# The split probabilities of a windowed attention laid side by side, the first operand of an output projection made earlier, and loads moved

## The chip, the cores and the metric

The kernel runs on one core of a Trainium2 chip. Its metric is the device time of one execution in microseconds (us), as the median of several runs; the slowest core counts, and here there is only one.

## The reference, cut to what matters

One layer of a hybrid encoder for 2048 prompt tokens and 64 decode tokens, 1024 wide. Attention (8 heads in 2 groups of 4, heads 64 wide, in chunks of 64 tokens, each of which sees its own chunk and the two before it) and a retention (4 heads, 128 wide) read one projection of the normed input. Their outputs go through one output projection, and a squared-ReLU MLP follows.

```python
a = _rmsnorm(hp, norm1[l])
qa, ka, va, qr, kr, vr, gr = _project(a, w_in[l], pos_p)      # rotates qa, ka, qr, kr
attn_o = _swa_prompt(qa, ka, va, sinks[l])
ret_o, s_p = _retention_prompt(qr, kr, vr)
hp = hp + _mix_out(attn_o, ret_o, gr, w_out[l])
hp = hp + _sqrelu_mlp(_rmsnorm(hp, norm2[l]), w_up[l], w_down[l])
...
def _attend(q, k, v, sinks, mask):
    s = jnp.einsum('...qkgd,...skd->...kgqs', q, k).astype(jnp.float32) * (HEAD_DIM ** -0.5)
    ...
    m = jnp.maximum(jnp.max(s, axis=-1), sink)
    p = jnp.exp(s - m[..., None])
    denom = jnp.sum(p, axis=-1) + jnp.exp(sink - m)
    p = (p / denom[..., None]).astype(v.dtype)
    o = jnp.einsum('...kgqs,...skd->...qkgd', p, v)
```

The attention has a band: for a tile of 128 tokens (two chunks) the keys are those of the tile before and of the tile itself, 256 columns, of which chunk 0 sees columns 0 to 192 and chunk 1 columns 64 to 256.

## The kernel before

All products are made from split operands: a float32 value is written as a high part that the fast matmul format holds exactly, and a low part, the rest. ScalarE (ACT) makes the high part by a copy, VectorE (DVE) the low part by a subtraction, and three matmuls per 128 rows of depth take the place of one. What the names mean: `xh` and `xl` are the split x, `w_1_1_5` is the split weight block 5 of column group 1 in the second phase, `raw`, `wraw` and `waraw` are weight blocks as loaded, `z` is the projection of a tile.

The first stage runs over 17 tiles (16 of 128 prompt tokens, and the decode tile of 64, whose low part lies beside the high one, so that it takes two matmuls per depth) in two phases, each for one half of the heads: in a phase every tile goes through three column groups of 384, 512 and 512 columns (`CN`). Group 0 holds the attention's values, keys and queries, groups 1 and 2 the retention's. The decode tile and the first prompt tile are done first, group by group in turn. The loop at L658 to L690 walks the groups; `group` (L549) issues the 24 (16) matmuls of one.

Behind the groups run the stages of the attention, `att_a` to `att_e` (L240 to L354): rotation and split of values and queries into `hl` (a value block is 128 columns, high and low parts beside each other), the transposes of queries and keys (`pq`, `pk`, into `qT` and `kw`), scores and softmax (`att_c`, L274), the transposes of the probabilities into `pt` and their split into `ph` and `pl` (`att_d`, L321), and the product with the values into `po` (`att_e`, L339). `att_c` writes the probabilities of a chunk at their place among the 256 columns and clears the 64 columns that the chunk doesn't see; `att_d` transposes all 256 columns of both chunks and both head pairs, that is eight blocks of 128 x 128 in two PSUM tiles. The retention stages are `ret_*`: `qk` is its rotated input, `ptr` the transposes of it, copied to `rkT`; `pss` are its scores, `pr` its product, `sd` its state, and `vs` and `sig` its values and gate.

The order of work on TensorE (PE) and on the DMA queue of SyncE (SP) is that in which the code issues it (L583); on the other engines a scheduler arranges it by a simulation of their times. A planner (`run_ready`, L531) puts the attention and retention stages between the matmuls of the groups: a stage is ready a time `LAT` after the stages that it needs, and adds `COST` to its clock. Nearly all loads go out on SP's queue, one behind the other, each waiting until its buffer is free and the eighth load before it has landed.

The start (L585 to L621) warms PE with 18 matmuls and issues the loads of the first group's weights (`load_w`, L115), of the x parts of the first two tiles (`load_part`, L591), of the second group's weights, of `rd`, of the token-wise x for the norm (`xk`) and the rotation table (`rt`, `load_aux`), and of the third group's weights, whose last loads borrow buffers of the attention stages, `ph` and `pl`. `token_norm` (L180) computes a tile's norm factor from `xk`.

At the change of phase, `load_ahead` (L123) loads the first blocks of a column group's next weights before the last group that uses the old ones, and `weights` splits them behind it. `load_x` (L146) loads a tile's x into `xr`, a single buffer, which GpSimd (POOL) leaves last, when it has made `xl`. Tile (1, 1) is the first of the second phase that is loaded anew; its load is issued at the group with the number `change + 7`.

The output projection (`out_part`, L764) forms eight blocks of 128 output columns d from eight blocks of mixed heads, in passes over 704 tokens, two halves of 352 each: 24 matmuls `y` per half. `wo` is the split operand, loaded and split one block ahead by `load_wout` (L754); `mhl` are the split mixed heads. Its first pass starts while the last tiles' attention is still under way: `run_ready` stands before each depth step until `phase1_done` (L852), which empties the stage queue. It is called behind the second output block (d = 1), by the hooks at L863.

## Time and profile before

| | |
|---|---|
| median of 3 runs | 2221.25 us (2221.06 to 2223.52) |
| profiled execution | 2221.45 us |
| its span | 2219.7 us |
| instructions | 35656 |
| VectorE busy | 1466.4 us (66%) |
| ScalarE busy | 1115.6 us (50%) |
| GpSimd busy | 444.8 us (20%) |
| mean DMA rate over the span | 232 GB/s |

The span runs from the first to the last instruction of the profiled execution; what lies around it makes the rest of its time. An engine's busy time is the sum of its instructions; two engines may be busy at once, so these times don't add up. The largest groups of instructions are TensorE's matmuls of the MLP, which stand behind the output projection and are not touched by the change.

### The profile page before, as it was taken

The numbers are of one execution on the slowest core, as the hardware profiler recorded it, in microseconds if no ns is written. First come the engines' busy times: TensorE is split into PE (matmuls) and PEld (weight loads), VectorE is DVE, ScalarE is ACT, GpSimd is POOL, SyncE is SP. The second block draws the span as 40 slices with busy tenths as digits, with TensorE's granted clock in tenths as the row PEclk, the third lists the DMA queues.
The fourth block names the chain that finished last, engine by engine and source line by source line (L and its number), as shares of the span: only waits on it lengthen the run. The fifth ranks groups of instructions, "written<-read, shape, count | busy, mean of one in ns | idle before, by whom it ended". The sixth has DMA issues, their size and how long they took to land.

```text
span 2219.7 us, 35656 instructions
## 1 busy us (share of the span) xinstructions
PE 2196.7 (99%) x13274; PEld 2108.1 (95%) x13274; DVE 1466.4 (66%) x2461; ACT 1115.6 (50%) x1983; POOL 444.8 (20%) x547
## 2 busy tenths in 40 slices
PE   8999999999999999999999999999999999999998
PEld 7888898888888999999999999999999999999998
DVE  6565557555456576787688668667666876677664
ACT  6444445444444433455565556555554444554452
POOL 4554444444443212100000000000001200120011
PEclk9999999999999999999999999999999999999999
DMA  6567964598554779489799779676976787777662
GB/s 184 163 182 186 249 173 151 166 221 204 138 124 132 263 264 336 151 306 347 237 322 350 258 234 323 228 231 215 361 263 226 269 290 239 234 275 271 239 211 81
DMA packets 240878, 515.92 MB, mean 232 GB/s; under 512 B 20144, under 2 KB 126320, under 8 KB 236608
## 3 DMA queue, kind: packets, MB, share of 16 engines
q1 hardware_dynamic: 231616, 469.62, 62.4%
q0 software_dynamic: 8512, 43.29, 9.3%
q8 instruction: 104, 1.70, 0.3%
q10 hardware_dynamic: 576, 0.72, 0.1%
q14 instruction: 70, 0.57, 0.1%
HBM read 411.19 MB, written 169.54 MB: 262 GB/s over the span
## 4 chain that ended last, share of the span: by engine, by line
PE 95%; DMA 2%; DVE 1%; issue 1%; ACT 1%; SPq 0%; POOL 0%; DVEq 0%; ACTq 0%; POOLq 0%
PE y L1094 9%; PE y L1093 9%; PE y L1092 9%; PE z L559 7%; PE z L560 7%; PE z L562 7%; PE b L922 4%; PE b L921 4%; PE b L920 4%; PE y L783 3%; PE y L785 3%; PE y L784 3%; PE a L922 3%; PE a L921 3%; PE a L920 3%; PE c L922 3%
## 5 line engine op out<-in xcount | busy, mean ns | idle before, releaser
L1094 PE MATMUL y<-vh,wd 128*128 128x352 f32 x1344 | 434.5, 323 | 0.5 <-DVE wd L496 0.5
L1093 PE MATMUL y<-vl,wd 128*128 128x352 f32 x1344 | 433.8, 323 | 0.0
L1092 PE MATMUL y<-vh,wd 128*128 128x352 f32 x1344 | 431.9, 321 | 0.0
L559 PE MATMUL z<-w,xh 128*128 128x512 f32 (+1 forms) x816 | 324.9, 398 | 1.4 <-ACT w L88 1.1
L1042 POOL TENSOR_TENSOR acc<-acc,sq 128x352 f32<-128x352 f32 x41 | 72.0, 1756 | 1212.2 <-ACT sq L1038 1212.2
L560 PE MATMUL z<-w,xh 128*128 128x512 f32 (+1 forms) x816 | 308.4, 378 | 1.1 <-DVE w L89 1.1
L495 ACT ACTIVATE wd<-dr 128x1024 fp32r<-128x1024 f32 x168 | 177.5, 1057 | 249.4 <-PE y L1094 171.7
L495 ACT ACTIVATE wu<-upr 128x512 fp32r<-128x512 f32 x336 | 209.2, 627 | 177.0 <-PE b L922 87.3
L562 PE MATMUL z<-w,xl 128*128 128x512 f32 (+1 forms) x768 | 288.9, 376 | 0.1
L496 DVE TENSOR_TENSOR wu<-upr,wu 128x512 fp32r<-128x512 f32 x336 | 231.2, 694 | 70.7 <-ACT wu L495 56.5
L496 DVE TENSOR_TENSOR wd<-dr,wd 128x1024 fp32r<-128x1024 f32 x168 | 209.2, 1247 | 95.6 <-ACT wd L495 95.6
L1094 PEld LDWEIGHTS y<-vh,wd 128*128 128x128 f32 x1344 | 252.8, 188 | 0.8 <-DVE wd L496 0.8
L1092 PEld LDWEIGHTS y<-vh,wd 128*128 128x128 f32 x1344 | 252.4, 188 | 0.0
L1093 PEld LDWEIGHTS y<-vl,wd 128*128 128x128 f32 x1344 | 252.4, 188 | 0.0
L921 PE MATMUL b<-al,wu 128*128 128x352 f32 x576 | 186.0, 323 | 0.0
L922 PE MATMUL b<-ah,wu 128*128 128x352 f32 x576 | 185.7, 323 | 0.0
L920 PE MATMUL b<-ah,wu 128*128 128x352 f32 x576 | 185.1, 322 | 0.0
L560 PEld LDWEIGHTS z<-w,xh 128*128 128x128 f32 x816 | 156.4, 192 | 20.6 <-DVE w L89 3.7
L559 PEld LDWEIGHTS z<-w,xh 128*128 128x128 f32 x816 | 156.4, 192 | 19.0 <-ACT w L88 1.6
L496 DVE TENSOR_TENSOR vl<-rv,vh 128x1408 fp32r<-128x1408 f32 x84 | 138.2, 1647 | 44.3 <-ACT vh L495 43.8
L562 PEld LDWEIGHTS z<-w,xl 128*128 128x128 f32 x768 | 145.0, 189 | 22.1 <-DVE xl L164 0.4
L495 ACT ACTIVATE vh<-rv 128x1408 fp32r<-128x1408 f32 x84 | 116.1, 1382 | 62.1 <-DMA rv<-vscr 44.9
(289 smaller groups left out, 4731.6 us busy)
## 6 DMA issues: line engine op xcount, KB each, us to landing
rv<-vscr SPq DMA_DIRECT2D x84, 704.0 KB, 5.5
vscr<-C SPq DMA_DIRECT2D x48, 1056.0 KB, 5.7
upr<-uscr SPq DMA_DIRECT2D x192, 256.0 KB, 5.1
dr<-sscr SPq DMA_DIRECT2D x96, 512.0 KB, 4.7
upr<-in_wup SPq DMA_DIRECT2D x144, 256.0 KB, 3.6
dr<-in_wdn SPq DMA_DIRECT2D x72, 512.0 KB, 5.2
uscr<-in_wup POOLq DMA_DIRECT2D x16, 1024.0 KB, 9.5
sscr<-in_wdn POOLq DMA_DIRECT2D x16, 1024.0 KB, 8.9
```

What stands on the lines that cost most here:

```text
L495: nc.scalar.activation(h, x, AF.Copy)
L496: nc.vector.tensor_sub(l, x, h.bitcast(F32))
L559: nc.tensor.matmul(z[:, :n], xh[:, k], wh, start=k == 0, stop=False)
L560: nc.tensor.matmul(z[:, :n], xh[:, k], wl, start=False, stop=k == NK - 1 and xl is None)
L562: nc.tensor.matmul(z[:, :n], xl[:, k], wh, start=False, stop=k == NK - 1)
L920: nc.tensor.matmul(o, wh, ah[:, k], start=k == 0 and i in (1, 6, 5), stop=False, skip_group_check=True)
L921: nc.tensor.matmul(o, wh, al[:, k], start=False, stop=False, skip_group_check=True)
L922: nc.tensor.matmul(o, wl, ah[:, k], start=False, stop=k == 3 and i in (2, 4, 3), skip_group_check=True)
L1042: nc.gpsimd.tensor_add(self.acc, self.acc, sq)
L1092: nc.tensor.matmul(o, wh, vh, start=f == 0, stop=False)
L1093: nc.tensor.matmul(o, wh, vl, start=False, stop=False)
L1094: nc.tensor.matmul(o, wl, vh, start=False, stop=f == 15)
```

## The change

**Attention.** The probabilities `p` of a head pair now lie in 384 columns, chunk 0 in 0 to 192 and chunk 1 in 192 to 384, so that there are no unseen columns, and the two memsets go. Three transposes of 128 columns serve a head pair instead of four: the first 128 columns (chunk 0 with the tile before), the last 128 (chunk 1 with this tile), and the middle 128, in which the upper 64 rows of the transpose belong to chunk 0 and the lower 64 to chunk 1. The former two go to `pt`, the middle one to `pm`. The middle rows are split in halves: in the new tile `pm`, one half of the 128 partitions holds the high part and the other the low part. A new tile `vd` holds the matching 64 rows of the values twice, once in each half of the partitions, made in `att_a` by copies on ACT and DVE. `att_e` now forms each chunk's `po` from three matmuls of 256 columns instead of both chunks' from four of 512. The planner's `COST` of `att_d` and `att_e` is lowered.

**Start.** The loads of the gains and of the decode tile's two x parts go out on ACT's DMA queue; on SP's queue all eight weight loads of the second group stand before `xk`, `rt` and `rd`. The borrowed buffers of the third group's loads are now one of `ph`, `pl`, `pm` and `p` each.

**Phase change.** The load of tile (1, 1)'s x is issued right behind `load_ahead(1)`.

**Output projection.** The first `wo` is loaded and split behind the last use of the second column group in phase 1, into buffers that the x tiles used (`xl`, `xk`, and `xr` for the raw load). `phase1_done` is called behind the third output block instead of the second.

```diff
-    nc.sync.dma_start(gsb, gains)
+    nc.scalar.dma_start(gsb, gains)
...
-            wk.tile([128, 512], F32, name="waraw", tag=tag, bufs=2) if tag else \
+            wk.tile([128, 2, 384 if tag == "p" else 256], F32, name="waraw", tag=tag).rearrange("p a n -> p (a n)") if tag else \
...
+        c.vd_prev = att[ph, t - 1].vd if 0 < t < NT - 1 else None
+        vd = c.vd = wk.tile([128, 2, 128], F32R, name="vd", bufs=3)
...
+        for a in range(c.nch):
+            v = hl[64 * a:64 * a + 64, 0:128].bitcast(F32)
+            nc.scalar.activation(vd[64 * (1 - a):128 - 64 * a, a], v, AF.Copy)
+            nc.vector.tensor_copy(vd[64 * a:64 * a + 64, a], v)
...
-        p = a.p = wk.tile([128, 2, 2, 256], F32, name="p")
+        p = a.p = wk.tile([128, 2, 384], F32, name="p")
...
-        if t > 0:
-            nc.gpsimd.memset(p[:, 0, :, 192:256], 0.0)
-            nc.gpsimd.memset(p[:, 1, :, 0:64], 0.0)
-        else:
-            nc.gpsimd.memset(p[:, 0, :, 192:256], 0.0)
...
     def att_d(a):
-        a.parts = []
-        nu = 2 * a.nch
-        for j in range(0 if a.t > 0 else 1, 2):
-            K = 128 if j == 0 else a.T
-            pt = psum("pt")
-            for c in range(a.nch):
-                for pr in range(2):
-                    v = 2 * c + pr
-                    nc.tensor.transpose(pt[:K, v * 128:v * 128 + 128], a.p[:, c, pr, j * 128:j * 128 + K], idf)
-            th = wk.tile([128, 512], F32R, name="ph", bufs=2)
-            tl = wk.tile([128, 512], F32R, name="pl", bufs=2)
-            nc.scalar.activation(th[:K, :nu * 128], pt[:K, :nu * 128], AF.Copy)
-            nc.vector.tensor_sub(tl[:K, :nu * 128], pt[:K, :nu * 128], th[:K, :nu * 128].bitcast(F32))
-            vv = (a.hl_prev if j == 0 else a.hl)[:K, 0:128]
-            a.parts.append((vv, th[:K, :nu * 128]))
-            a.parts.append((vv, tl[:K, :nu * 128]))
+        a.parts = [[], []]
+        n, t = a.nch, a.t
+        full = [c for c in range(n) if c == 1 or t > 0]
+        f0, f1 = full[0] * 256, full[-1] * 256 + 256
+        K = 128 if n == 2 and t > 0 else 64
+        pt, pm = psum("pt"), psum("pm")
+        for c in full:
+            for pr in range(2):
+                v = 2 * c + pr
+                nc.tensor.transpose(pt[:, v * 128:v * 128 + 128], a.p[:, pr, 256 * c:256 * c + 128], idf)
+        for pr in range(2):
+            nc.tensor.transpose(pm[:K, pr * 128:pr * 128 + 128], a.p[:, pr, 128:128 + K], idf)
+        th = wk.tile([128, 512], F32R, name="ph")
+        tl = wk.tile([128, 512], F32R, name="pl")
+        tm = wk.tile([128, 2, 256], F32R, name="pm")
+        nc.scalar.activation(th[:, f0:f1], pt[:, f0:f1], AF.Copy)
+        nc.vector.tensor_sub(tl[:, f0:f1], pt[:, f0:f1], th[:, f0:f1].bitcast(F32))
+        for c in full:
+            vv = (a.hl if c else a.hl_prev)[:, 0:128]
+            a.parts[c] += [(vv, x[:, 256 * c:256 * c + 256]) for x in (th, tl)]
+        for c in range(K // 64):
+            h, l = tm[64 * c:64 * c + 64, c], tm[64 * (1 - c):128 - 64 * c, c]
+            x = pm[64 * c:64 * c + 64, 0:256]
+            nc.scalar.activation(h, x, AF.Copy)
+            nc.vector.tensor_sub(l, x, h.bitcast(F32))
+            a.parts[c].append(((a.vd_prev if c else a.vd)[:, c], tm[:, c]))
 
     def att_e(a):
...
-        for i, (l, r) in enumerate(a.parts):
-            nc.tensor.matmul(po[:, :nu * 128], l, r, start=i == 0, stop=i == len(a.parts) - 1)
+        for c in range(nch):
+            for i, (l, r) in enumerate(a.parts[c]):
+                nc.tensor.matmul(po[:, 256 * c:256 * c + 256], l, r, start=i == 0, stop=i == len(a.parts[c]) - 1)
...
-    COST = dict(att_b=0.35, att_c=0.85, att_d=0.88, att_e=0.86, ret_b=0.44, ret_c=0.44, ret_d=1.3, ret_e=0.22)
+    COST = dict(att_b=0.35, att_c=0.85, att_d=0.66, att_e=0.72, ret_b=0.44, ret_c=0.44, ret_d=1.3, ret_e=0.22)
...
-        nc.sync.dma_start(xraw[n][:, k:k + 4, :T], xt[:, k:k + 4, t0:t0 + T] if T == 128 else xd[:, k:k + 4])
-
-    raws = []
-    for k in range(NK):
-        raws.append(load_w(0, 0, k, True))
-        if k < 2:
-            load_part(0, 4 * k)
+        (nc.sync if n else nc.scalar).dma_start(xraw[n][:, k:k + 4, :T], xt[:, k:k + 4, t0:t0 + T] if T == 128 else xd[:, k:k + 4])
+
+    for k in range(2):
+        load_part(0, 4 * k)
...
+    raws = [load_w(0, 0, k, True) for k in range(NK)]
...
-    raws = [load_w(0, 1, k, True) for k in range(4)]
+    raws = [load_w(0, 1, k, True) for k in range(NK)]
+    xs[a] = [*x0, load_aux(*a)]
     nc.sync.dma_start(rd, rdec)
-    xs[a] = [*x0, load_aux(*a)]
-    raws += [load_w(0, 1, k, True) for k in range(4, NK)]
...
-    raws = [load_w(0, 2, k, tag=(None, None, None, "ph", "ph", "pl", "pl")[k]) for k in range(NK - 1)]
+    raws = [load_w(0, 2, k, tag=(None, None, None, "ph", "pl", "pm", "p")[k]) for k in range(NK - 1)]
...
             raws = load_ahead(ci)
+            if ci == 1:
+                n = len(xs)
+                assert tiles[n] == (1, 1) and n not in xraw
+                xraw[n] = load_x(1)
...
+            raw = xp.tile([128, 1024], F32, name="wo0raw", tag="xr", bufs=1)
+            nc.sync.dma_start(raw, wout[0])
+            for a in range(2):
+                w = xp.tile([128, 2, 512], F32R, name="wo0", tag=("xl", "xk")[a], bufs=2 - a)
+                first_wo.append((w[:, 0], w[:, 1]))
+            for a in range(2):
+                split(*first_wo[a], raw[:, a * 512:a * 512 + 512])
...
-    wnext.append(load_wout(0))
+    wnext.append(first_wo)
     hooks = {d: [later(next_mix, 1, 2 * (d - 2) + k) for k in range(2)] for d in range(2, 6)}
-    hooks[1] = [phase1_done]
+    hooks[2].insert(0, phase1_done)
```

How instructions stand on an engine is shown at three places; a row gives the line, the operation, out<-in, and partitions x elements, with x and a count for rows in a series.

SP's queue at the start, in the kernel before (`gsb` are the gains, `xr` x for the matmuls, `xd` that of the decode tile, `xk` x by tokens for the norm):

```order
L63 DMA gsb<-in_gains 128x24
L120 DMA wraw<-in_w 128x384
L593 DMA xr<-in_xd 128x256
L120 DMA wraw<-in_w 128x384
L593 DMA xr<-in_xd 128x256
L120 DMA wraw<-in_w 128x384 x6
L593 DMA xr<-in_xt 128x4x128 x2
L120 DMA wraw<-in_w 128x512 x4
L607 DMA rd<-in_rdec 128x8
L172 DMA xk<-in_xtok 64x1024
L174 DMA rt<-in_rot 64x384
L120 DMA wraw<-in_w 128x512 x4
```

And in the changed kernel:

```order
L118 DMA wraw<-in_w 128x384 x8
L608 DMA xr<-in_xt 128x4x128 x2
L118 DMA wraw<-in_w 128x512 x8
L170 DMA xk<-in_xtok 64x1024
L172 DMA rt<-in_rot 64x384
L623 DMA rd<-in_rdec 128x8
L118 DMA raw<-in_w 128x512 x3
L118 DMA waraw<-in_w 128x512 x4
```

The gains and the decode tile's x parts have left the queue; the eight 128x512 loads stand together, and `xk`, `rt` and `rd` behind them, where `xk` stood in their middle. Those three loads stand at the head of ACT's order in the changed kernel, ahead of its first computation:

```order
L63 DMA gsb<-in_gains 128x24
L608 DMA xr<-in_xd 128x256 x2
L613 ACT_TABLE_LOAD
L613 ACTIVATE first<-mhalf 128x3
L86 ACTIVATE w_0_0_0_154<-wraw,gsb 128x384
L161 ACTIVATE xh<-xr 128x4x64
```

SP's queue at the change of phase, before:

```order
L120 DMA raw<-in_w 128x384 x8
L120 DMA raw<-in_w 128x512 x3
L128 DMA xk<-in_w 128x2x512
L120 DMA raw<-in_w 128x512 x3
L152 DMA xr<-in_xt 128x8x128
L120 DMA raw<-in_w 128x512 x3
L128 DMA xk<-in_w 128x2x512
L120 DMA raw<-in_w 128x512 x3
```

And in the changed kernel:

```order
L118 DMA raw<-in_w 128x384 x8
L118 DMA raw<-in_w 128x512 x3
L126 DMA xk<-in_w 128x2x512
L150 DMA xr<-in_xt 128x8x128
L118 DMA raw<-in_w 128x512 x6
L126 DMA xk<-in_w 128x2x512
L118 DMA raw<-in_w 128x512 x3
```

The x load (`xr`) stands right behind the load of two blocks at once (`xk<-in_w`) of the second column group, ahead of the last three blocks of that group.

PE in the output projection, before, around the last attention (of the decode tile: `prt` and `pt` transposes, `po` its product, `y` the output projection):

```order
L785 MATMUL y<-mhl,wo 128x352
L435 MATMUL prt<-idf,ro 128x64 x2
L330 MATMUL pt<-idf,p 128x128 x2
L330 MATMUL pt<-idf,p 64x128 x2
L344 MATMUL po<-ph,hl 128x256
L783 MATMUL y<-mhl,wo 128x352
```

And in the changed kernel, where each "..." leaves out rows of `y`, 22, 25 and 7 of them:

```order
L450 MATMUL prt<-idf,ro 128x64 x2
L810 MATMUL y<-mhl,wo 128x352
...
L812 MATMUL y<-mhl,wo 128x352
L335 MATMUL pt<-idf,p 128x128 x2
L337 MATMUL pm<-idf,p 64x128 x2
L810 MATMUL y<-mhl,wo 128x352
...
L812 MATMUL y<-mhl,wo 128x352
L359 MATMUL po<-ph,hl 128x256
L810 MATMUL y<-mhl,wo 128x352
...
L359 MATMUL po<-pl,hl 128x256
L812 MATMUL y<-mhl,wo 128x352
L359 MATMUL po<-pm,vd 128x256
```

Before, transposes and product stood in a row with nothing between them; now 24 `y` matmuls stand between `prt` and `pt`, 27 between `pm` and the first `po`, and the three `po` come apart. ACT at the start of the output projection, before:

```order
L495 ACTIVATE mhl<-mraw 128x704 x3
L567 ACTIVATE zb<-z 64x512
L495 ACTIVATE mhl<-mraw 128x704
L308 ACTIVATE p,sm<-s,ngm 128x192 x4
L312 ACTIVATE es<-es 128x4
L385 ACTIVATE rkT<-ptr 128x256
L367 ACTIVATE vs<-z,rsv 128x128 x2
L372 ACTIVATE sig<-z,hrs 128x256
L567 ACTIVATE zb<-z 64x512
L495 ACTIVATE wo<-woraw 128x512 x4
L411 ACTIVATE ro,s_8143<-pr 128x128 x2
```

And in the changed kernel:

```order
L510 ACTIVATE mhl<-mraw 128x704 x2
L510 ACTIVATE wo_8129<-wo0raw 128x512
L510 ACTIVATE wo_8130<-wo0raw 128x512
L510 ACTIVATE mhl<-mraw 128x704
L582 ACTIVATE zb<-z 64x512
L510 ACTIVATE mhl<-mraw 128x704
L309 ACTIVATE p,sm<-s,ngm 128x192 x4
L313 ACTIVATE es<-es 128x4
```

The first operand's high parts (`wo_8129`, `wo_8130`) now stand among the splits of the mixed heads, ahead of the last group's copies `zb`; before, the four `wo` splits (of the first two operands) stood behind the softmax (`p`, `es`) and the retention's copies.

## The prediction

> **What bounds the kernel now.** I read the page first, then the waits of TensorE (PE), then short windows around each wait for the granted clock.

> ```profile
> span 2219.7 us, 35656 instructions
> PE 2196.7 (99%) x13274; PEld 2108.1 (95%) x13274; DVE 1466.4 (66%) x2461; ACT 1115.6 (50%) x1983; POOL 444.8 (20%) x547
> ```

> The first line is the span of the profiled execution; its time is 2221.45 us, so 1.75 us lie around the span. It stands 0.2 us from the median of the three runs (2221.25), and I make the sum against 2221.45. PE is busy 2196.7 of 2219.7 us. Only two things can shorten this kernel: less work on PE, or fewer of the few holes in it.

> ```profile
> PE pss L391 <- ACT rkT L385: 3.6, 1, 3.6
> PE ptr L380 <- POOL qk L217: 1.3, 1, 1.3
> PE y L783 <- ACT wo L495: 1.3, 1, 1.3
> PE z L559 <- ACT w L88: 1.1, 1, 1.1
> PE pt L330 <- DVE p L319: 1.1, 1, 1.1
> PE z L560 <- DVE w L89: 1.1, 3, 0.5
> ```

> A row gives who waited for whom, then total us, count and longest. Before the final norm these are nearly all of PE's waits, each in one of three places: the start (z L559, z L560, ptr), the change from the first half of the columns to the second (pss), and the start and end of the stage in which the last attention stands between the first output projection's matmuls (y, pt). A hole also costs what comes behind it:

> ```profile
> 18.00:22.00 4.00, 2.31 (x6) 1.06 (x5) 2.34 (x6) 3.35 (x8) 1.85 (x4) 0.90 1.04 370
> 22.00:28.00 6.00, 5.51 (x14) 3.93 (x13) 6.00 (x10) 5.53 (x10) 6.00 (x3) 0.50 1.01 346
> 364.00:368.20 4.20, 0.60 (x4) 0.28 (x3) 3.26 (x8) 3.50 (x9) 2.40 (x2) 1.00 0.63 172
> 368.20:372.60 4.40, 4.40 (x21) 4.40 (x22) 4.40 (x9) 2.85 (x6) 1.11 (x2) 0.63 0.84 281
> 711.00:718.00 7.00, 5.53 (x26) 4.52 (x25) 3.68 (x8) 3.05 (x8) 0.39 (x1) 0.76 0.95 202
> 738.00:741.00 3.00, 1.68 (x12) 1.05 (x10) 1.36 (x6) 2.15 (x9) 1.36 (x2) 1.00 0.32 105
> 741.00:745.00 4.00, 4.00 (x16) 4.00 (x17) 0.71 (x3) 0.85 (x3) 1.10 (x1) 0.57 0.95 296
> ```

> Columns: window and length, busy time (and instructions) of PE, PE's weight loads, VectorE (DVE), ScalarE (ACT), GpSimd (POOL), then PEclk, DMA share, GB/s. After each hole the granted clock is about half for some us: 0.50 from 22 to 28, 0.63 behind the 3.6 us, 0.57 behind the 1.3 us at 738. Idle time plus (1 - clock) x busy time is what a place loses. At full clock a z matmul follows the last after 0.23 us (99.01 to 99.23 below), so the 6 + 14 that start between 18 and 28 are worth 4.6 us and take 10: **5.4 us** lost, and 1.3 more at ptr. The phase change loses 3.6 + 0.37 x 4.4 = **5.2 us**. The output projection loses 1.5 + 0.24 x 5.5 = 2.8 us at its start and 1.3 + 0.43 x 4 = 3.0 us at 738 to 745, **5.8 us**. Elsewhere PE has work without a break, so a shorter instruction there is a shorter run.

> **The change part by part.**

> *Attention, all 34 tiles.* Before, a full tile is 8 transposes and 4 matmuls of 512 columns; now 6 transposes and 6 matmuls of 256.

> ```profile
> 97.90 1.03 PE L330 MATMUL pt<-idf,p 128*128 128x128 f32 x8
> 98.69 0.48 PE L559 MATMUL z<-w,xh 128*128 128x512 f32 x1
> 99.01 0.39 PE L560 MATMUL z<-w,xh 128*128 128x512 f32 x1
> 99.23 0.40 PE L562 MATMUL z<-w,xl 128*128 128x512 f32 x1
> ...
> 108.40 0.39 PE L344 MATMUL po<-ph,hl 128*128 128x512 f32 x1
> ...
> 109.33 0.34 PE L559 MATMUL z<-w,xh 128*128 128x384 f32 x1
> ```

> The eight transposes run from 97.90 to 98.69, and the z matmul behind takes 0.32 instead of 0.23: (0.79 + 0.09) / 8 = 0.11 us each, two gone = 0.22 us. The four wide matmuls take 109.33 - 108.40 = 0.93 us. A 256-wide one stands only in the decode tile:

> ```profile
> 66.26 0.28 PE L344 MATMUL po<-ph,hl 128*128 128x256 f32 x1
> 66.38 0.28 PE L344 MATMUL po<-pl,hl 128*128 128x256 f32 x1
> 66.58 0.38 PE L344 MATMUL po<-ph,hl 64*128 64x256 f32 x1
> 66.81 0.28 PE L344 MATMUL po<-pl,hl 64*128 64x256 f32 x1
> 67.01 0.45 PE L559 MATMUL z<-w,xh 128*128 128x384 f32 x1
> ```

> Between two with 128 rows of weights (`128*128`) 0.12 us pass; where 64 rows follow or precede, 0.20 to 0.22. In the new form the middle block's values and its split probabilities fill all 128 partitions, so I take 0.12: 6 x 0.12 = 0.72, and 0.93 - 0.72 = 0.21 us saved. The 30 full tiles give 30 x (0.22 + 0.21) = 12.9 us. The two first tiles keep four transposes and go from 2 x 0.23 to 3 x 0.12, 0.1 us each; the two decode tiles go from 0.75 (66.26 to 67.01) to 0.36, 0.4 us each. Together **13.9 us**; I take 13.4, since one interval carries the 0.12 and a switch of shape costs a few hundredths. Bounds: 12 to 15.

> ACT and DVE get two 64-partition casts each per tile, and four half-size operations in place of two full ones; POOL loses two memsets. All that lies beside PE as long as nothing is late. In a steady tile:

> ```profile
> 515.81 1.29 DVE L334 TENSOR_TENSOR pl<-pt,ph 128x512 fp32r<-128x512 f32 x2 [0.39 <-ACT ph L333]
> ```
> ```profile
> 520.59 0.39 PE L344 MATMUL po<-ph,hl 128*128 128x512 f32 x1
> ```

> DVE ends the split at 517.10 and PE starts on it at 520.59: 3.5 us of cover, against at most two more ACT copies and DVE subtractions of 0.6 us. I cost it at nothing; without that cover each us would cost a us, per tile.

> *The first operand of the output projection.* Its load and split now stand in front of the last group of matmuls. ACT and DVE have 8 splits there already, and two more of each (about 0.6 us each) fit before PE needs them. What is late next is qk of the decode tile, whose rotation stands behind the two splits on DVE; I see some 0.4 us of room. The forced emptying of the attention queue moves one output block later, so that a block of y matmuls stands between prt, pt and po (the rows of order above): pt's wait on p goes. Of the 5.8 us and the few tenths around them I take **6.0**; bounds 4 to 6.6.

> *The x load moved up.*

> ```profile
> 362.25 0.73 ACT L88 ACTIVATE w<-raw,gsb 128x512 fp32r<-128x512 f32 x1 [0.96 <-DMA raw<-in_w]
> ...
> 365.25 1.06 ACT L163 ACTIVATE xh<-xr 128x1024 fp32r<-128x1024 f32 x1 [0.70 <-DMA xr<-in_xt]
> 366.21 0.61 ACT L367 ACTIVATE vs<-z,rsv 128x128 f32<-128x128 f32 x2
> ...
> 367.68 0.39 ACT L385 ACTIVATE rkT<-ptr 128x256 f32<-128x256 f32 x1
> ```

> rkT, for which PE waits, stands behind xh on ACT, and xh waits for its load. With the load issued ahead of three weight loads (5 to 7 of the second column group), xh no longer waits, but the weight split of 362.25 waited for its own load, and those now stand behind the x load on SP's queue; the x load itself waits until POOL has left its buffer. In the new order ACT does, from 362.25, one weight split, xh, vs, sig, a weight split, a half copy and rkT: 0.65 + 0.95 + 0.5 + 0.35 + 0.62 + 0.45 + 0.4 = 3.9, so rkT is there at 366.2 instead of 368.07. **1.9 us**, and the half clock behind it stays. Bounds: 0 (the weight loads come later by the x load's 1.9) to 5.2.

> *The start.*

> ```profile
> 10.80 0.56 SPq L172 DMA_DIRECT2D xk<-in_xtok  x1
> ...
> 12.09 4.43 SPq L120 DMA_DIRECT2D wraw<-in_w  x4
> ```
> ```profile
> 18.66 1.06 ACT L184 ACTIVATE xk<-xk 64x1024 f32<-64x1024 f32 x1 [0.65 <-DMA xk<-in_xtok]
> ...
> 26.00 1.93 ACT L88 ACTIVATE w<-waraw,gsb 128x512 fp32r<-128x512 f32 x3
> ```
> ```profile
> 24.16 2.06 DVE L89 SCALAR_TENSOR_TENSOR w<-raw,gsb,w 128x512 fp32r<-128x512 f32 x3
> ...
> 30.50 0.54 DVE L251 TENSOR_TENSOR hl<-zr,hl 64x384 fp32r<-64x384 f32 x1
> ```
> ```profile
> 32.02 0.22 PE L228 MATMUL pk<-idr,hl 128*128 128x128 f32 x1
> ...
> 38.02 0.46 PE L380 MATMUL ptr<-idf,qk 64*128 64x64 f32 x4 [1.29 <-POOL qk L217]
> ```

> Before, xk (10.80) is issued between the fourth and the fifth weight load of the second column group and takes until 18.66; loads five to eight (from 12.09) come behind it, and PE starves from 18 to 28. Now xk comes behind all eight, and the x parts of the first tile and the gains go out on ACT's queue. So PE should run through the second group without a hole and stand at pk (32.02) about 7 us earlier, near 25. But pk needs hl, and hl the weight splits of the third group ahead of it in order on ACT and DVE. The bytes up to the seventh of those loads are the same; its split was the last of the three from 26.00 on ACT. DVE was behind by then (hl ended at 31.04); with no idle time earlier it should end the seventh split near 27.3 and hl near 28, and pk should run at 28.5: 3.5 us. The rest of the chain (first split of the next tile, rotation, qk) keeps its length, so ptr still waits. PE then idles some 3 us at pk, and of the gain I let a slower clock take a quarter: **2.6 us**. Bounds: all of it (5.4 + 1.3 = 6.7), and -1.7, as in the stretch 741 to 745, if the order brings nothing and one more half-clock stretch comes.

> The sum: 13.4 + 6.0 + 1.9 + 2.6 = 23.9 us, and 2221.45 - 23.9 = **2197.5 us**.

> **The rivals.**

> 1. *A new wait in every tile* (slower). PE's po waits for the last of the four half copies. For it: they are shorter but more, and ACT does ro between the two. Against it: 3.5 us of cover. The chain would have to grow by 3.5 us before PE waits at all, and by 4.5 before the 23.9 us are eaten: 30 waits of 1 us would lose 30 us and give some 2227, more with the half clock that followed the 1.3 us at 738. From 0.95 us of wait per tile on ((23.9 + 4.4) / 30) it is slower. Chance 0.04.
> 2. *The narrow matmuls are no cheaper.* If each takes the 0.20 to 0.22 us of the rows at 66.38 and 66.58, six take 1.26 us instead of 0.93, and a tile gains 0.22 - 0.33 = -0.11. Then attention costs 3 us and the time is 2221.45 - 10.5 + 3 = 2214. Against it: those rows change between 128 and 64 rows of weights. Chance 0.06.
> 3. *The clock takes the start back.* PE comes to pk early, waits a whole stretch, and runs at half clock behind it; the start gives -1.7 instead of 2.6 and the time is 2201.8. For it: 1.3 us were enough at 738 for 1.7 us of loss. Against it: PE waits at pk for DVE anyway, so slow matmuls behind pk are partly hidden under the wait at ptr. Chance 0.2. [...]
> 4. *All holes close.* The phase change gives 5.2 and the start 6.7: 2190.1. Against it: the chain over hl and rkT above. Chance 0.08.

> **How the numbers follow.** The forecast, 2197.5 with its terms within their middle bounds (2192.5 to 2201), has 0.62. To hold the time 8 times in 10 the range takes in rival 3 and most of the bounds between rival 4 and it: 2191 to 2204.5. A measurement of this kernel tells some 0.2% (4.4 us) from no change. Faster by more: the forecast and rivals 2, 3 and 4, 0.96 (2214 is still faster by 7 us). Rival 1 is the rest: slower 0.03, within 0.2% 0.01.

> **What would show each step.** Attention: pt and pm x6 in 0.66 us, po x6 in 0.72 us, a steady tile shorter by 0.4 us, and no PE wait on pm or vd. Output projection: no wait of y for wo, none of pt for p, clock 1.0 from 690 to 740. Phase change: xh without a DMA wait ahead of it, pss waiting about 2 us. Start: no wait of z for w from 17 to 25, a wait of pk for hl, ptr some 3 us earlier. I am wrong if po intervals are near 0.2 us, if PE waits in the steady tiles, or if the start is no earlier at ptr.

## The result, and the profile after

The changed kernel takes 2203.9 us (median of 4 runs, 2201.29 to 2204.97) against 2221.34 us before (4 runs, 2221.06 to 2223.52): ratio 0.9917, 95% interval 0.9905 to 0.9930. Its profiled execution is the fastest of the four: 2201.29 us. The forecast was 2197.5. First the page and TensorE's waits in the changed kernel.

```profile
span 2199.5 us, 35734 instructions
PE 2178.0 (99%) x13274; PEld 2096.7 (95%) x13274; DVE 1493.8 (68%) x2559; ACT 1141.5 (52%) x2081; POOL 428.4 (19%) x481
```
```profile
PE pss L406 <- ACT rkT L400: 4.1, 1, 4.1
PE pk L226 <- DVE hl L467: 3.4, 1, 3.4
PE y L812 <- DVE wo L511: 0.9, 1, 0.9
PE ptr L395 <- POOL qk L215: 0.3, 1, 0.3
```

PE is busy 18.7 us less, and most of the holes have other names. pk and pss wait 3.4 and 4.1 us; the long waits of z for weights at the start, and that of pt in the output projection, are gone; y waits 0.9 us for the low part of wo.

To set the places beside each other I cut every trace at the same instructions, with the groups of z matmuls numbered from 0: the *start* from the first z matmul to group 9, the *phase change* from group 50 to group 58, and the *output projection* from the middle of group 99 to the 481st y matmul. These are the rows of the kernel before (columns as in the prediction: window and length, PE busy, weight loads, DVE, ACT, POOL, PEclk, DMA share, GB/s):

```profile
5.94:65.73 59.79, 55.95 (x253) 44.36 (x254) 38.87 (x80) 33.21 (x82) 29.27 (x37) 0.94 0.64 194
352.45:412.53 60.08, 56.48 (x319) 50.46 (x318) 39.16 (x87) 32.69 (x85) 26.12 (x29) 0.97 0.46 138
698.58:805.54 106.96, 104.17 (x618) 98.61 (x618) 64.62 (x117) 52.15 (x106) 24.91 (x26) 0.97 0.68 227
```

Of the changed kernel:

```profile
6.28:63.85 57.57, 53.67 (x252) 43.57 (x253) 39.53 (x86) 35.09 (x88) 25.74 (x36) 0.97 0.62 193
344.25:404.94 60.69, 56.55 (x319) 50.84 (x318) 40.98 (x95) 34.50 (x93) 23.54 (x24) 0.94 0.45 140
684.83:786.15 101.32, 100.21 (x618) 95.03 (x617) 66.19 (x120) 52.99 (x109) 26.81 (x27) 1.00 0.70 243
```

And of the same kernel in a later execution:

```profile
5.64:64.95 59.31, 55.43 (x254) 45.66 (x254) 38.80 (x86) 35.04 (x88) 25.14 (x36) 0.94 0.61 191
345.39:406.39 61.00, 56.86 (x319) 51.16 (x318) 41.53 (x95) 34.54 (x93) 23.49 (x24) 0.94 0.46 141
686.28:787.81 101.53, 100.11 (x618) 95.06 (x617) 66.01 (x120) 52.99 (x109) 25.95 (x27) 1.00 0.70 240
```

The length less PE's busy time is idle time; what the half clock costs while PE is busy I take from the clock records behind PEclk. These begin only at 10.95 us in the kernel before and at 9.1 to 13.4 us in the others. Ahead of them the z matmuls of 384 columns follow each other after 0.32 us (9.10 to 9.42 in the kernel before), behind them after 0.17 (11.00 to 11.17), so the clock is half there too; that loss is in none of the figures. Start: 59.8, 57.6 and 59.3 us (idle 3.8, 3.9, 3.9; half clock 3.1, 1.7, 3.4). Phase change: 60.1, 60.7 and 61.0, **longer** than before although its tiles have become shorter (idle 3.6, 4.1, 4.1; half clock 1.7, 2.7, 3.0). Output projection: 107.0, 101.3 and 101.5 (idle 2.8, 1.1, 1.4; half clock 3.4, 0, 0). Between these places, some 82 groups without a hole, 12.5 us went (from 65.73 to 352.45 and 412.53 to 698.58 before; 63.85 to 344.25 and 404.94 to 684.83 now), 0.46 us for each three groups.

Attention, a steady tile of the changed kernel:

```profile
504.74 0.60 PE L335 MATMUL pt<-idf,p 128*128 128x128 f32 x4
505.17 0.38 PE L337 MATMUL pm<-idf,p 128*128 128x128 f32 x2
...
510.56 0.28 PE L359 MATMUL po<-ph,hl 128*128 128x256 f32 x1
510.67 0.28 PE L359 MATMUL po<-pl,hl 128*128 128x256 f32 x1
510.79 0.28 PE L359 MATMUL po<-pm,vd 128*128 128x256 f32 x1
...
511.15 0.28 PE L359 MATMUL po<-pm,vd 128*128 128x256 f32 x1
```

The six matmuls follow each other after 0.11 to 0.12 us, as the forecast had it, and nothing waits for pm or vd.

### The profile page after: what moved, and what is told of

It is laid out like the page before. It is cut to its first block, busy times and chain, and to the rows that moved or that the text cites. A ratio compares the mean times of both kernels' runs of the same rounds, so it can differ in the third digit from the quotient of the medians.

```text
span 2199.5 us, 35734 instructions
## 1 busy us (share of the span) xinstructions
PE 2178.0 (99%) x13274; PEld 2096.7 (95%) x13274; DVE 1493.8 (68%) x2559; ACT 1141.5 (52%) x2081; POOL 428.4 (19%) x481
## 4 chain that ended last, share of the span: by engine, by line
PE 95%; DMA 2%; issue 1%; ACT 1%; DVE 1%; POOL 0%; SPq 0%; ACTq 0%; DVEq 0%; POOLq 0%
PE y L1121 10%; PE y L1120 10%; PE y L1119 10%; PE z L574 7%; PE z L575 7%; PE z L577 7%; PE b L949 4%; PE b L948 4%; PE b L947 4%; PE y L810 3%; PE c L949 3%; PE a L949 3%; PE y L812 3%; PE a L948 3%; PE c L948 3%; PE y L811 3%
```

## The experiments

All kernels ran in 4 or 5 timed runs beside the kernel before on the same chip (its medians there 2220.7 to 2221.5; the attention alone and the three undone parts on another chip than the later ones). The intervals are 0.13% (2.8 us) to each side, so the medians don't separate most of these kernels. I read the lengths of the three places instead, from one profile of each; two profiles of the same kernel, the first two rows, already differ by 1.1 us at group 9 and by 0.3 and 0.2 in the other places. "Gain at group 9" is how much earlier group 9 starts than in the kernel before.

| kernel | median us | ratio (95% interval) | gain at group 9 | phase change | output projection |
|---|---|---|---|---|---|
| changed | 2203.9 | 0.9917 (0.9905 to 0.9930) | 1.9 | 60.7 | 101.3 |
| changed, again | 2203.9 | 0.9927 (0.9913 to 0.9940) | 0.8 | 61.0 | 101.5 |
| attention alone | 2206.4 | 0.9935 (0.9922 to 0.9947) | -0.5 | 59.4 | 103.2 |
| x load undone | 2205.3 | 0.9926 (0.9914 to 0.9938) | 2.3 | 60.2 | 101.2 |
| start undone | 2206.5 | 0.9934 (0.9922 to 0.9947) | -0.9 | 61.2 | 102.8 |
| output projection undone | 2206.2 | 0.9932 (0.9919 to 0.9946) | 0.9 | 61.2 | 106.3 |
| weights-first undone | 2205.0 | 0.9931 (0.9918 to 0.9945) | -0.8 | 60.8 | 101.4 |
| keys later | 2206.7 | 0.9937 (0.9925 to 0.9950) | 4.3 | 60.7 | 102.4 |
| filler before keys | 2204.1 | 0.9919 (0.9905 to 0.9932) | -0.9 | 61.6 | 101.9 |
| rkT on VectorE | 2202.3 | 0.9920 (0.9907 to 0.9934) | 0.6 | 59.0 | 101.2 |
| rkT on VectorE, x load undone | 2203.7 | 0.9916 (0.9902 to 0.9930) | -0.4 | 60.2 | 101.9 |
| three waits filled | 2205.0 | 0.9924 (0.9910 to 0.9938) | 0.7 | 61.7 | 100.3 |
| rkT and wo | 2203.9 | 0.9921 (0.9907 to 0.9934) | -0.6 | 60.6 | 100.8 |

**The changed kernel again.**

> The changed kernel once more, unaltered. Theory: the waits of TensorE repeat within 0.3 us (pk 3.4, pss 4.1, y for wo 0.9), but the half-clock stretches behind them do not: at the start one or two of 3.4 us, in the output projection none to two; so the profiled time lies anywhere between 2200 and 2206 us, and the median near 2204. Rival: the profiled 2201.3 is typical and the three slower runs were not: median below 2202.

The waits repeat (pk 3.5, pss 4.1, y 0.9), the half clock does not: from its rows above, the start has PEclk 0.94 instead of 0.97. By the trace's clock records one half-clock stretch of 3.41 us followed pk's wait in the first execution (31.13 to 34.54), and 6.83 us in the second (29.51 to 36.33). The profiled times are 2201.29 and 2203.63. So 2201.3 was the lucky end of eight runs, and the second execution, near the median, has one stretch (1.7 us) more. The executions that weren't profiled may differ elsewhere.

**Attention alone.** The kernel before with the new attention stages, their buffers and their `COST`, and no other part of the change.

> The kernel before with the attention part alone (start, x load and output projection as before). Theory, from the interval between like matmuls in the two traces: a full tile gains 0.44 us and all of the attention 14.3, so 2221.3 - 14.3 = 2207.0 us, and in its trace the 3.6 us wait of pss and the waits of the output projection are still there. The forecast's term was 13.4: 2207.9. Rival: some of what the trace books under attention comes from the other parts; then it is nearer 2210.

2206.4 us, 15 us below the kernel before, as expected. The surprise is the output projection, whose code is unchanged here: 103.2 us instead of 107.0.

```profile
PE y L800 <- ACT wo L512: 1.3, 1, 1.3
PE pt L337 <- DVE p L323: 1.0, 1, 1.0
```
```profile
685.92:789.07 103.15, 100.45 (x617) 95.03 (x617) 66.30 (x120) 53.10 (x109) 26.42 (x27) 1.00 0.70 236
```

The waits are those of before (1.3 for wo, 1.0 for p), but PEclk is 1.00 where it was 0.97: no half clock followed.

**Output projection undone.**

```diff
-    wnext.append(first_wo)
+    wnext.append(load_wout(0))
...
-    hooks[2].insert(0, phase1_done)
+    hooks[1] = [phase1_done]
```

> The changed kernel without the early first operand and with the stage queue emptied one block earlier, as before. Theory: the part is worth 5.6 us by the traces, 6.0 by the forecast: 2209.5 to 2209.9 us, with y waiting for wo about 1.3 us and pt for p about 1 us, each with a half-clock stretch. Rival: with the shorter attention tail the waits shrink and it is worth under 4 us: below 2208.

```profile
PE y L801 <- ACT wo L510: 1.3, 1, 1.3
PE pt L335 <- DVE p L321: 1.0, 1, 1.0
```
```profile
686.44:792.75 106.31, 103.60 (x618) 98.11 (x618) 66.63 (x120) 53.11 (x109) 26.40 (x27) 0.97 0.69 231
```

The waits of before are back with the same sizes, and there are two half-clock stretches of 3.41 us again, 3.4 us lost. Only the first (702.16 to 705.57) stands behind one of the waits, that of y. The second (722.64 to 726.05) ends 2.1 us ahead of pt's wait (728.19 to 729.17); in the 3.4 us before it PE was never idle, but for the most part (719.31 to 722.28) ran short products and transposes, most of them the decode tile's. Median 2206.2, below the 2209.5 expected and below 2208, as the rival had it. In the profiled executions the part removes 1.6 us of idle time (106.31 - 103.60 = 2.7 here, 101.32 - 100.21 = 1.1 with it). That is the better end: in seven of the eleven profiles with the new order a wait of 0.2 to 1.4 us for a later wo follows at 740 to 744 us, and in the nine with this order of y the idle time of the place is 1.1 to 2.7 us, 1.7 in the mean. Half-clock stretches stood in this place in two of three profiles of the old order and in none of the eleven of the new one. The two edits in it weren't tried apart.

**Start undone, and weights-first undone.** The second puts xk, rt and rd back between the fourth and fifth weight load, and leaves the gains and the decode tile's x on ACT's queue:

```diff
-    raws = [load_w(0, 1, k, True) for k in range(NK)]
-    xs[a] = [*x0, load_aux(*a)]
+    raws = [load_w(0, 1, k, True) for k in range(4)]
     nc.sync.dma_start(rd, rdec)
+    xs[a] = [*x0, load_aux(*a)]
+    raws += [load_w(0, 1, k, True) for k in range(4, NK)]
```

> The changed kernel with the loads of the start as before. Theory, from the traces: the start gives 1.9 us at the eighth group of matmuls, since pk waits 3.4 us for hl and the half clock follows; so 2203.9 + 1.9 = 2205.8 us, with the waits of z for w and of ptr for qk (1.3 us) back. Rival: the start is worth its whole 6 us in most executions and the profiled one was not typical: 2210.

> The changed kernel; the gains and the decode tile's x stay on ACT's queue, but xk, rt and rd stand again between the fourth and the fifth weight load of the second group. Theory: the order of the weights carries the start; z waits for w again by some 2 us from 18 to 22 us, ptr for qk by over 1 us, and the gain at the eighth group of matmuls falls from about 1.7 us (0.9 to 2.3 in three executions) to that of the undone start (-0.9 to -0.5). Rival: the second queue carries it, and the gain stays over 1.5 us.

```profile
PE ptr L395 <- POOL qk L215: 2.4, 1, 2.4
PE z L574 <- ACT w L86: 1.9, 1, 1.9
PE z L575 <- DVE w L87: 1.3, 2, 1.0
```

Both lose the gain, -0.9 and -0.8 us at group 9, and in both z waits for weights and ptr for qk again (rows of the second: 3.2 and 2.4 us). So by these waits the order of the weights carries the start; the second queue alone shows nothing. Both medians (2206.5 and 2205.0) lie above the changed kernel's, by 1 to 2.6 us.

**Keys later.** Is the wait at pk only a matter of what stands first on PE?

```diff
-        return None if any(x is None for x in ts) else max(ts)
+        return None if any(x is None for x in ts) else max(ts) + {('att_b', 0): 3.0, ('ret_b', 0): 5.0}.get((name, n), 0.0)
```

> The changed kernel; the planner is told that the decode tile's keys and queries are ready 3 us later and its retention transposes 5 us later, so that pk, pq stand behind seven of the eight weight blocks of the third group, and ptr behind six blocks of the next tile. Theory: the 3.4 us wait of pk is only a matter of what stands first on TensorE, since seven split weight blocks of the third group are there by 28.7 us; the wait goes down to some 1.5 us (the eighth block is split at 30.9), and the half clock behind it with it: 2 to 5 us gained, 2199 to 2202 us. Rival: the chain that follows (rotation, qk, ptr) sets the time whatever stands before it, ptr then waits what pk did: under 1 us.

```profile
PE z L574 <- DVE sig L389: 2.5, 3, 1.6
PE pk L226 <- DVE hl L467: 0.2, 1, 0.2
```

This pk no longer waits (0.2 us), and group 9 starts 3.5 us earlier than in the changed kernel's second execution. Then the lead is lost: at group 50 this kernel stands 2.7 us *behind* it, and the median is 2206.7, where 2199 to 2202 was expected. z now waits for DVE (sig above all) here and there until 96 us. I put that down to the planner, whose clock moved with the delay so that later stages came closer together, but tried nothing to show it. The first half of the theory held; the sum went to the rival's side, though the wait that came was not ptr's.

**Filler before the keys.** Matmuls that nobody reads, to keep PE from being idle:

```diff
+        if (c.ph, c.t) == (0, NT - 1):
+            idle = psum("idle")
+            for _ in range(18):
+                nc.tensor.matmul(idle[:, 0:384], idr, ws[0, 0][0][:, 0], start=True, stop=True)
```

> The changed kernel with 18 matmuls of 384 columns that compute nothing needed, in the hole ahead of pk at the start (18 x 0.173 = 3.1 us of the 3.4 to 4.0 us wait). Theory: the hole itself stays, but TensorE is not idle in it, so the half clock from 30 us on (one or two stretches of 3.4 us, 1.7 us of loss each) goes: the gain at the eighth group of matmuls rises from 0.6 to 2.3 us to 3.5 or more, and the time falls by 1 to 3 us from 2203.9 and spreads less. Rival: the clock does not look at this wait, or the filler delays pk: no gain, or slower by up to 1 us.

```profile
PE ptr L399 <- POOL qk L215: 1.6, 1, 1.6
PE pk L226 <- DVE hl L471: 1.0, 1, 1.0
```

```profile
30.23 0.54 DVE L251 TENSOR_TENSOR hl<-zr,hl 64x384 fp32r<-64x384 f32 x1
```

The half clock from 30 us on was gone, and the start was no earlier for it: ptr waited 1.6 us for qk, where the changed kernel waits 0.3, and a half-clock stretch followed that (38.83 to 42.24). The gain at group 9 is no clean measure here, since hl came late in this execution (30.77, row above) for reasons ahead of the filler; it came at 29.27 and 29.38 in the two of the changed kernel. Counted from hl, ptr came 6.6 us later here, 6.9 and 7.8 there, so the full clock brought ptr forward by 0.3 and 1.3 us, until it waited for qk; in the second execution, with 6.83 us of half clock, ptr waited for nothing and PE itself was late. The stretch behind the new wait took it back: counted from hl, group 6 started 15.6 us later here, 14.3 and 15.3 there. The median, 2204.1, shows no gain either.

**x load undone.**

```diff
-            if ci == 1:
-                n = len(xs)
-                assert tiles[n] == (1, 1) and n not in xraw
-                xraw[n] = load_x(1)
```

> The changed kernel with the x load of tile (1, 1) where it was. Theory A, from the trace of the changed kernel: the moved load delays the three weight loads behind it by its own 2.2 us, ACT still splits two of them ahead of xh, so rkT came 0.5 us later against PE and the half clock behind it lasted longer; without the move the run gains 1.6 us (2203.9 to 2202.3), and pss waits 3.6 us instead of 4.1. Theory B, the forecast: the move is worth 1.9 us, 2205.8 and a longer wait. Theory C: the wait is the same within 0.2 us, since the same loads and splits stand ahead of rkT either way, and the time is 2203.9 within the spread.

```profile
PE pss L406 <- ACT rkT L400: 4.5, 1, 4.5
```
```profile
343.91:404.07 60.16, 55.63 (x319) 49.92 (x318) 41.13 (x95) 34.59 (x93) 23.34 (x24) 0.97 0.48 143
360.70:364.11 3.41, 3.41 (x16) 3.41 (x15) 3.14 (x5) 2.22 (x5) 0.88 (x1) 0.50 0.87 269
```

None of the three as stated. PE waits longer without the move (4.5 against 4.1 us), against theory A; the move does bring rkT 0.4 us earlier, though the second of the three weight loads behind it lands 1.2 us later (by the traces 12.0 us behind the start of group 50, 10.8 without the move). But the half clock behind the wait lasts 3.41 us (360.70 to 364.11) without the move instead of 6.83 (358.81 to 365.63), and the place is 0.5 to 0.8 us shorter. In all seven profiles with the load moved and rkT on ACT the half clock lasted 6.83 us, and the place 60.7 to 61.6 us, mean 61.0; in the two with it unmoved and the new attention 3.41 us, and 59.4 and 60.2. So in the profiles, seven against two, the place is about 1.3 us longer with the move, where the forecast had a gain of 1.9. The medians lean the other way (2205.3 here, 2203.9 with the move) and the ratios not at all (0.9926 here, 0.9917 and 0.9927), and the profiled run here was the fastest of its five. So it isn't shown whether the move gains or costs; a gain of 0.4 us in PE's wait is what the traces show.

**rkT on VectorE.** What holds pss? The timelines of PE, ACT and SP in the changed kernel (start, us, instruction; in brackets the idle time before it and what ended it):

```profile
351.16 0.60 PE L395 MATMUL ptr<-idf,qk 128*128 128x128 f32 x4
...
360.25 1.22 PE L406 MATMUL pss<-rqT,rkT 128*128 128x128 f32 x4 [4.14 <-ACT rkT L400]
```
```profile
354.18 0.72 ACT L86 ACTIVATE w<-raw,gsb 128x512 fp32r<-128x512 f32 x1 [0.82 <-DMA raw<-in_w]
356.23 0.72 ACT L86 ACTIVATE w<-raw,gsb 128x512 fp32r<-128x512 f32 x1 [1.33 <-DMA raw<-in_w]
356.86 1.04 ACT L161 ACTIVATE xh<-xr 128x1024 fp32r<-128x1024 f32 x1
...
358.66 0.72 ACT L86 ACTIVATE w<-raw,gsb 128x512 fp32r<-128x512 f32 x1
359.40 0.38 ACT L349 ACTIVATE pm<-pm 64x256 fp32r<-64x256 f32 x1
359.81 0.38 ACT L400 ACTIVATE rkT<-ptr 128x256 f32<-128x256 f32 x1
```
```profile
349.08 0.56 SPq L150 DMA_DIRECT2D xr<-in_xt  x1
349.74 11.49 SPq L118 DMA_DIRECT2D raw<-in_w  x6
```

The transposes run at 351.16 and end at 351.8; the x load goes out at 349.08, ahead of the loads of the last blocks. rkT stands in ACT's queue behind the splits at 354.18 and 356.23, each of which waits for its load (0.82 and 1.33 us), behind xh, and behind a third split. So I let DVE copy that one rkT, right behind rqT.

```diff
-        nc.scalar.activation(c.rkT[:, :, :T], pv[:, 2:4], AF.Copy)
+        if (c.ph, t) == (0, NT - 2):
+            nc.vector.tensor_copy(c.rkT[:, :, :T], pv[:, 2:4])
+        else:
+            nc.scalar.activation(c.rkT[:, :, :T], pv[:, 2:4], AF.Copy)
```

> The changed kernel; for the prompt tile 15 of the first phase alone, whose pss TensorE waits for, the copy rkT is made by DVE right behind rqT instead of by ACT. Theory: the transposes for rkT end at 351.8 us and rkT waits 8 us in ACT's queue behind weight splits, xh, vs and sig; on DVE it is there at about 355.9, pss doesn't wait over 0.3 us, and TensorE waits next for the split x of tile (1, 1) (xh 357.9, xl 360.3 us), some 1.5 us; 4.1 - 1.5 = 2.6 us gained, and up to 1.7 of half clock: 2199.7 to 2201.3 us from 2203.9. Rival: the wait is set by the loads, and z of tile (1, 1) waits as long as pss did: under 1 us gained.

```profile
PE z L580 <- POOL xl L162: 1.8, 1, 1.8
PE z L577 <- ACT xh L161: 0.4, 1, 0.4
```
```profile
345.57:404.53 58.96, 56.57 (x320) 49.87 (x318) 42.11 (x96) 34.27 (x92) 23.34 (x24) 0.97 0.47 146
```

pss's wait is gone and z waits 1.8 us for xl and 0.4 for xh, as the theory had it (it said some 1.5 us), with 59.0 us for the place. Median 2202.3 (2201.75 to 2202.87), against 2203.2 to 2204.29 for the changed kernel in the same session: 1.6 us gained, where 2.6 or more were expected. ACT's order held pss: with rkT taken out of it, pss doesn't wait.

**The same with the x load unmoved.**

> The changed kernel with rkT of the prompt tile 15 of the first phase on DVE, and the x load of tile (1, 1) where it was before the change. Theory: the moved load is worth something only once pss no longer waits for rkT, since then z of tile (1, 1) waits for xh and xl; with the load back, xh starts no earlier than the landing of x (in the unmoved runs some 13 us behind the first wide weight load), so z waits for xl 2 to 4 us instead of 1.8, and the run is 0.5 to 2 us slower than the one with the load moved (2202.3): 2202.8 to 2204.3. Rival: the load's place does not matter here either, xh stands behind the same weight splits: the same within 0.3 us in the waits.

60.2 us for the place, and 2203.7, both 1.2 to 1.4 us more than with the move, as the theory had it, but PE's wait fell on pss (1.9 us, for a rkT that DVE itself made late) and pm (1.1), not on xl. And the kernel with the move varies as much: with the load moved and the same rkT on DVE, the last experiment has 60.6 us for the place.

**Three waits filled, and rkT and wo.** Products with the low part, which comes last, stand behind those with the high part: for z of tile (1, 1) and for y of the second output block in the first, for y alone in the second. The y part of the edit, without the line that takes these products out of the loop above it:

```diff
+                if (p, d, b) == (0, 1, 0):
+                    for f in range(8):
+                        wl, mh = w[f // 4][1][:, f % 4 * 128:f % 4 * 128 + 128], mix[f][:, 0, cs]
+                        nc.tensor.matmul(po[:, :NB], wl, mh, start=False, stop=f == 7)
```

> The changed kernel with rkT of that one tile on DVE, and two orders of matmuls altered where the operand that comes last is the low part: the products of z of tile (1, 1), group 0, with xl stand behind the 16 with xh, and those of the second output block's first half with the low part of wo behind the 16 with the high part. Theory: with xl last, z no longer waits 1.8 us for it (16 x 0.173 = 2.8 us of cover), and y no longer 0.9 us for wo; 2202.3 - 2.7 = 2199.6 us, and up to 1.7 less where the half clock behind these waits goes too. Rival: another operand of the same place comes as late (xh, a weight block), and under 1 us is gained.

> The changed kernel with rkT of that one tile on DVE and the second output block's low-part products behind the 16 with the high part; z of tile (1, 1) as it was. Theory: the stretch of the phase change is that of the run with rkT on DVE alone (a gain of some 0.9 us from the group at 353 us to that at 404 us against the kernel before, where the changed kernel loses 0.8 to 1.1), and y doesn't wait for wo: 1.1 us less between the 48th and the 72nd y matmul, as in the run with three orders altered. 2202.3 - 1.1 = 2201.2 us, and below both kernels. Rival: with rkT on DVE the stretch varies by 2 us from run to run, and the time is 2203 to 2204 as for the changed kernel.

Waits of PE in the first, then in the second:

```profile
PE pq L270 <- DVE sm L314: 2.0, 1, 2.0
PE po L359 <- DVE pm L350: 1.2, 1, 1.2
```
```profile
PE pk L226 <- DVE hl L470: 4.7, 1, 4.7
PE z L580 <- POOL xl L162: 1.8, 1, 1.8
PE pt L335 <- DVE p L321: 1.6, 2, 1.1
```

In the first, z waits for nothing and the output projection is the shortest of all, 100.3 us; but the phase change is the longest, 61.7: pq waits 2.0 us and po 1.2 for DVE (rows above), which split weight blocks shortly before (the last one ahead of po's pm from 360.79 to 362.30). In the second, y's wait is gone again (100.8 us), but with rkT on DVE the phase change takes 60.6 us, not 59.0, and pk waits 4.7 us at the start. So rkT on DVE is not a settled gain; of the three only the order of y helped both times, and both medians (2205.0 and 2203.9) miss the expected 2199.6 and 2201.2. No version is shown to beat the changed kernel: the best median, 2202.3, has an interval of 0.9907 to 0.9934.

## Why the prediction was right in direction and range, and 6.4 us off

The kernel is faster, and 2203.9 us lies in the range of 2191 to 2204.5. It does not lie in the band of the forecast itself, 2192.5 to 2201, which had 0.62: the range, which had been widened for rival 3 (2201.8), holds it with 0.6 us to spare. The sum was made against the profiled execution, so I compare it with the changed kernel's own (2201.29).

| term | forecast | profile |
|---|---|---|
| attention | 13.4 | 14.0 |
| output projection | 6.0 | 5.1 |
| phase change, x load | 1.9 | -1.5 |
| start | 2.6 | 1.9 |
| behind the output projection | 0 | 0.7 |

- **Attention: right.** 12.5 us in the stretches without holes, 0.9 in the phase change (60.08 - 60.69, with holes and clock together 5.3 before and 6.8 now) and 0.6 in the output projection. The rule read from the decode tile's row, 0.12 us for 256 columns between full rows, held (0.11 to 0.12 us in the steady tile); rivals 1 and 2 did not come.
- **Output projection: size nearly right, its nature not.** pt's wait on p went, as said; y's wait for wo did not go but became one of 0.9 us for the next operand's low part. Of the 5.1 us, 3.4 are half-clock stretches, which the profile of the attention alone was free of too, without any edit to this code; that the size came out nearly right is to that extent luck.
- **Start: right in mechanism.** pk waits 3.4 us for hl (forecast: some 3), ptr 0.3. ptr came 1.9 and 0.8 us earlier in the two executions (36.13 and 37.23 against 38.02), not some 3. The size varies from execution to execution: -0.6 to 2.3 us at group 9 in the eight profiles with this start and nothing else altered there, 0.8 in the mean. hl ended between 28.9 and 30.7 us in them, and one or two half-clock stretches followed. The three with the old order of weights and the new attention lie at -0.9 to -0.5, so the part is worth some 1.5 us in the mean. Rival 3 comes true in part in most of these.
- **Phase change: the step that failed.** "In the new order ACT does, from 362.25, one weight split, xh, vs, sig, a weight split, a half copy and rkT": two weight splits stand ahead of xh, not one, and the one at 356.23 waited 1.33 us for a load that the x load had been put in front of. What the move brought is 0.4 us of PE's wait (4.5 us without it, 4.1 with it), not 1.9. The bound of 0, "the weight loads come later by the x load's 1.9", left out the half clock, which became twice as long: against the kernel before idle time +0.5 us, clock +1.0. The longer idle time isn't the move's, since the idle time of the place is 4.5 us with the load unmoved, against 4.1; what lengthened it, and whether the longer half clock is the move's, stays open.
- **Behind the output projection: spread.** The rest of the span takes 1413.3 to 1415.0 us in the fourteen profiles, so 0.7 us is no effect of the change that they show.
- **Not a term: the draw.** The sum fits one execution; the median is 2.6 us above the fastest one profiled. The profile of before, 0.2 us from its median, happened to be a typical draw, with five units of 3.41 us of half clock; the changed kernel's had three, its second execution four.

So 3.8 us of the miss to 2201.29 are 3.4 (phase change) + 0.9 (output projection) + 0.7 (start) - 0.6 (attention) - 0.7 (behind it), within rounding; the other 2.6 are the draw.

## What to carry to other kernels

Read what a late operand waits for from the queue of the engine that makes it, and count every instruction that stands ahead of it, with the load that each waits for: moving one load past others on a shared queue moved their waits here (1.33 us ahead of the split at 356.23), not only its own. The gain by shorter instructions on the busiest engine added up as forecast (14.0 us, forecast 13.4); a gain by closing holes was worth the hole and the clock behind it, and since that clock changed from one execution to the next (3.41 and 6.83 us of half clock behind the same wait of pk), it belongs in the range.

## What the runs showed of the hardware that I had not expected

Within an execution all stretches begin whole multiples of 3.413 us apart: in the kernel before at 21.19, 369.35, 714.10 and 741.40 us, which are 102, 101 and 8 multiples from one to the next. So I cut each trace into pieces at these multiples, ahead of the final norm, and took PE's idle time in each from the profile. Behind all 24 pieces at full clock with 1.75 us or more of it the clock was halved; with 1.3 to 1.7 us behind 7 of 18; with less behind two, one with 0.98 us and one with none, that of the short products in the undone output projection. In the kernel before, 1.63, 2.18, 1.47 and 1.32 us stood in the pieces ahead of its four stretches, and 1.42 us in one (362.53 to 365.94) that no stretch followed. How a wait fell on these pieces went with what came behind it: the changed kernel's first execution had pk's wait in two of them (1.70 and 1.75 us) and one unit of half clock, the second had it in one (3.41 us) and two units. That a wait costs less when it is split between two pieces was only read from the traces, not tested, and it doesn't always hold (rkT on VectorE, with a wait of 4.0 us: 2.01 and 2.02 us, two units).

Why the half clock behind pss lasted 6.83 us in all seven profiles with the x load moved and rkT on ACT, and 3.41 us in the three with it unmoved (the kernel before among them), is not settled. In the seven PE was still idle for 0.2 to 1.5 us of the first 3.41 us of half clock (1.44 us in the changed kernel), in the three for none; no run tried whether the one has to do with the other.
